# The tiles of the normed activations' high and low parts start 32 bytes further on

## The chip, the cores and the metric

The kernel runs on one core of a Trainium2 chip. The metric is the device time of one execution in microseconds; the times given are medians over runs. The core has a matrix engine (TensorE, in the profile PE for its matmuls and PEld for its weight loads), VectorE (DVE), ScalarE (ACT), GpSimd (POOL), and SyncE (SP), which issues most of the DMA transfers. All of them work on one on-chip memory of 128 partitions; a tile takes the same range of bytes in every partition.

## What is computed

The reference is one step of a trunk of two layers over 128 context tokens and 512 latent tokens of 1024 channels. The part that takes most of the time is the channel mixer at the end of each layer, which reads a table `u` and a table `v` of 16384 experts each:

```
h = rmsnorm(x, g_ffn) * (1 + scale) + shift
q = (h @ w_q).reshape(tokens, 8, 2, 128)            # 8 heads, 2 halves
s = einsum('thpc,hpnc->thpn', q, sub_keys)          # scores against 128 keys per half
sv, si = top_k(s, 16)
...                                                 # the best 16 pairs of keys: eidx, gates
act = gelu(einsum('thkd,td->thk', u[eidx], h))
x = x + gate * einsum('thk,thkd->td', gates * act, v[eidx])
```

Ahead of it layer 0 has an attention and a recurrence, fed by one projection of the normed activations, and layer 1 has a pooling mixer.

## The kernel before

Tokens lie along the free dimension: `xT` holds the 1024 channels as 8 blocks of 128 partitions, each with 640 tokens (128 context, 512 latent).

**Products in three parts.** Every large product is made with float32r operands split into a rounded high part and the low rest, as high x high, high x low and low x high (`PAIRS`, L367). The normed activations stand in two tiles, `hh` (high) and `hl` (low), 8 blocks of 640 tokens each; L496 to L500 write them. The weights are split as they come: `w_load` (L284) fetches 512 KB into `wr`, `w_hi` (L293) lets ACT write the high part `wh`, `w_lo` (L311) lets DVE or POOL write the rest `wl`. `mm3` (L369) goes through the 8 blocks of channels k, and for each k through the three pairs; the stationary operand is 128 columns of a weight tile, the moving operand a stretch of `hh` or `hl`.

**Where matmuls read `hh` and `hl`.**

- Projections in layer 0, output projection, pooling mixer, and the 16 query chunks of each channel mixer (L379, L528, L1397): moving operands of 320 tokens, two halves per weight column.
- The "U stage" of each channel mixer (L1546 to L1598): all 512 latent tokens are multiplied with all 16384 rows of `u`, 128 rows in each of 128 turns. A turn is 24 matmuls with 512 moving columns from `hh` and `hl`, summed in one bank (L1550). In half of the turns 16 pairs of small f16 matmuls (`pgm`, L1424, L1425) follow, which build the gate matrix out of one-hot rows that DVE and ACT make beside.
- The attention's value product (L893): here 128 columns of `hh` or `hl` are the stationary operand and 512 columns of a weight tile the moving one.

The "V stage" (L1617 to L1641) multiplies the gated activations, split into `wgh` and `wgl`, with `v`: 128 turns of 24 matmuls of 512 columns over 8 banks; its last turn (L1647 to L1650) goes bank by bank with the three pairs one after the other. It reads the gate matrix back into `gt_` in even groups of 8 turns and into the memory of `hl` in odd ones (L1510 to L1518), since the activations are no longer needed then.

**What sets the order.** In the U and V stages the loop itself is the order; each engine goes through its queue. In the other stages a planner (`Plan`) lists operations with estimated costs and writes them out in an order it searches for with a fixed seed; it knows nothing of addresses.

**Where the tiles lie.** Pool `pc` places its tiles in the order in which they are named, each padded to a multiple of 32 bytes. In the program of the kernel before, the starts are (bytes within a partition):

| tile | start | over a multiple of 64 | over a multiple of 512 |
|---|---|---|---|
| `hh`, `hl` | 51264, 71744 | 0 | 64 |
| `s8` (8 columns for the recurrence) | 92224 | 0 | 64 |
| `wr` (3), from pool `pw` | 92256, 96352, 100448 | 32 | 96 |
| `wh` (2), `wl` (2) | 104544, 108640; 112736, 116832 | 32 | 96 |
| `wh3`, `wl3` (third pair in the U and V stages) | 126560, 130656 | 32 | 96 |
| `gt_`, layers 0 and 1 | 192096, 181856 | 32 | 96 |
| `wgh`, layer 0 (2) | 212576, 214624 | 32 | 96 |
| `wgl`, layer 0 (2) | 216672, 218720 | 32 | 96 |

The `wgh` and `wgl` of layer 1 also stand 32 over a multiple of 64 and 96 over one of 512. Block k of `hh` starts 2560 k bytes on, its latent tokens 512 bytes later, its second half of 320 tokens 1280 bytes later, and the columns of a weight tile in steps of 512 bytes: all of these are multiples of 64, so that the third column of the table holds for every operand of these matmuls.

Of the kernel before, what the change touches and what calls it, by code (L numbers as in the profile page):

```python
# [11 lines left out]
F32 = mybir.dt.float32  # L12
# [144 lines left out]
def tile_trunk(ctx: ExitStack, tc: tile.TileContext, a, o):  # L157
# [5 lines left out]
    pc = ctx.enter_context(tc.tile_pool(name="pc", bufs=1))  # L163
# [12 lines left out]
    def col(name, j=None):  # L176
        s, w = COLS[name]
        return cols[:, s:s + w] if j is None else cols[:, s + j:s + j + 1]
# [57 lines left out]
    def norm_cols(l, part):  # L236
# [8 lines left out]
    perm = pc.tile([128, 128], F32, name="perm")  # L245
    eps = pc.tile([128, 1], F32, name="eps")
    warm = pc.tile([128, 1], F32, name="warm")
    G.iota(iota16, pattern=[[1, 128]], base=0, channel_multiplier=0,
           allow_small_or_imprecise_dtypes=True)
    G.memset(ones, 1.0)  # L250
# [293 lines left out]
    def lru_columns(pl):  # L544
        n = 8
        lam = col("lam")
        z = pl.tile([128, n], F32, name="lz")
        s = pl.tile([128, n], F32, name="ls")
        s2 = pl.tile([128, n], F32, name="ls2")
        q = pl.tile([128, n], F32, name="lq")  # L550
        S.activation(z, lam, AF.Abs)
        S.activation(z, z, AF.Exp, scale=-1.0)
        V.tensor_scalar(s, z, 2.0, None, op0=OP.add)
        V.reciprocal(s, s)
        V.tensor_tensor(s, s, z, op=OP.mult)
        V.tensor_tensor(s2, s, s, op=OP.mult)
        V.memset(q, 1.0 / 19)
        for k in range(8, -1, -1):
            V.tensor_tensor(q, q, s2, op=OP.mult)
            V.tensor_scalar(q, q, 1.0 / (2 * k + 1), None, op0=OP.add)  # L560
        V.tensor_tensor(q, q, s, op=OP.mult)
        V.tensor_scalar(s, lam, -1.0, 0.0, op0=OP.mult, op1=OP.max)
        s8 = pc.tile([128, n], F32, name="s8")
        V.scalar_tensor_tensor(s8, q, 2.0, s, op0=OP.mult, op1=OP.add)
        V.tensor_scalar(s8, s8, -8.0, None, op0=OP.mult)
        return s8

    def mixer0(p_mm, tmp, gt, firsts):
        NK = TP + 128 + TS
# [1104 lines left out]
    with tc.tile_pool(name="tmp", bufs=1) as tmp, tc.tile_pool(name="pmm", bufs=1, space=PSUM) as p_mm:  # L1674
        with tc.tile_pool(name="pm0", bufs=1) as pm0:
# [152 lines left out]
            for c in range(2):  # L1828
                wts.next()
            plan.run(S=1.5)  # L1830
            s8 = lru_columns(pm0)
        mixer0(p_mm, tmp, gt, firsts)
    A, B, gt = norm_cols(0, 1)
    peer(0, A, B, gt)
# [134 lines left out]
```

## Time and profile before

| | |
|---|---|
| median of 3 runs | 3773.19 us (3772.8 to 3774.68) |
| the profiled execution | 3772.78 us, of which its span is 3771.0 us |
| PE busy | 3622.1 us, 96% of the span |
| DVE busy | 2997.7 us, 79% |
| ACT, POOL busy | 1640.7 us, 828.3 us |
| granted clock of TensorE, mean | 0.98 |
| moved by DMA | 894.58 MB, mean 237 GB/s |

The profile is of one execution. Busy time is a union of spans; a matmul's span is longer than the distance to the next one, since they are pipelined, so what a stream of matmuls costs is read from the distance between starts. `idle before` is the time an engine stood still ahead of an instruction, with what ended it.

### The profile page before, as it was taken

How to read it: one execution, taken by the hardware profiler on the slowest of the kernel's cores; microseconds unless marked ns; L12 is line 12 of the kernel's file. 1: busy time of each engine (PE TensorE's matmuls, PEld its weight loads, DVE VectorE, ACT ScalarE, POOL GpSimd, SP SyncE). 2: the span in 40 equal slices, each digit the busy share in tenths (PEclk: the TensorE clock that was granted, in tenths of full speed). 3: DMA queues.
4: the chain of work that ended last, by engine and by line, in shares of the span. 5: the costliest groups of instructions: out<-in, count | busy, mean ns of one | idle time of the engine just before them, and what ended most of it. 6: DMA issues, size and time to landing. Idle time of an engine off the chain costs nothing. (4 is left out here: it accounts for less than half of the span.)

```text
span 3771.0 us, 52891 instructions
## 1 busy us (share of the span) xinstructions
PE 3622.1 (96%) x18190; PEld 2986.1 (79%) x18190; DVE 2997.7 (79%) x6901; ACT 1640.7 (44%) x2900; POOL 828.3 (22%) x673
## 2 busy tenths in 40 slices
PE   7989889999999999999996799999999999999997
PEld 5957888888888888888885797888888888888886
DVE  7876888888988778888887798988888656666665
ACT  3743323756657333333333323657566433333333
POOL 3122311111111412222213321111111322222221
PEclk9999899999999999999998899999999999999999
DMA  5233126878778999999991215878788978888883
GB/s 200 74 118 130 53 66 202 276 256 280 255 261 277 361 309 324 330 331 323 324 318 47 69 57 176 265 258 279 257 269 269 339 250 298 294 295 297 299 296 107
DMA packets 400162, 894.58 MB, mean 237 GB/s; under 512 B 33746, under 2 KB 170386, under 8 KB 399252
## 3 DMA queue, kind: packets, MB, share of 16 engines
q1 hardware_dynamic: 272884, 490.07, 40.5%
q0 software_dynamic: 74016, 271.09, 21.1%
q10 hardware_dynamic: 52992, 130.05, 8.8%
q8 instruction: 142, 2.33, 0.3%
q14 instruction: 128, 1.05, 0.1%
HBM read 758.26 MB, written 132.81 MB: 236 GB/s over the span
## 5 line engine op out<-in xcount | busy, mean ns | idle before, releaser
L315 DVE TENSOR_TENSOR wl<-wr,wh 128x1024 fp32r<-128x1024 f32 x544 | 660.4, 1215 | 546.7 <-ACT wh L306 470.5
L306 ACT ACTIVATE wh<-wr 128x1024 fp32r<-128x1024 f32 (+1 forms) x578 | 601.0, 1041 | 900.1 <-PE po L1632 735.8
L1288 POOL DMA_INDIRECT gat<-in_u_dram,idx x256 | 283.5, 1107 | 1285.4 <-DVE oh L1478 655.1
L1288 POOL DMA_INDIRECT gat<-in_v_dram,idx x256 | 303.6, 1186 | 1022.6 <-DVE accP L1610 957.4
L1632 PE MATMUL po<-wgh,wh 128*128 128x512 f32 x2032 | 501.9, 389 | 0.0
L1632 PE MATMUL po<-wgh,wl 128*128 128x512 f32 x2032 | 501.8, 389 | 0.0
L1632 PE MATMUL po<-wgl,wh 128*128 128x512 f32 x2032 | 501.8, 389 | 0.0
L1632 PEld LDWEIGHTS po<-wgh,wh 128*128 128x128 f32 x2032 | 381.4, 188 | 79.3
L1632 PEld LDWEIGHTS po<-wgl,wh 128*128 128x128 f32 x2032 | 381.4, 188 | 79.2
L1632 PEld LDWEIGHTS po<-wgh,wl 128*128 128x128 f32 x2032 | 381.4, 188 | 79.2
L1610 DVE SCALAR_TENSOR_TENSOR accP<-gat,aP,accP 128x1024 f32<-128x1024 f32 x254 | 324.8, 1279 | 0.5
L1480 DVE TENSOR_SCALAR oh<-iota,ij,gs 128x128 f16<-128x128 f16 x1024 | 321.9, 314 | 0.0
L1411 DVE SCALAR_TENSOR_TENSOR gat<-gat,hP 128x1024 f32<-128x1024 f32 x256 | 310.7, 1219 | 12.2 <-DMA gat<-in_u_dram,idx 12.2
L1419 ACT ACTIVATE oh<-oh,gs 128x128 f16<-128x128 f16 x1024 | 313.4, 387 | 0.0
L1478 DVE TENSOR_SCALAR oh<-iota,ij 128x128 f16<-128x128 f16 x1024 | 253.2, 247 | 0.0
L1542 ACT ACTIVATE wgh<-w 128x512 fp32r<-128x512 f32 x256 | 161.8, 632 | 206.6 <-PE po L1632 205.2
L1544 DVE TENSOR_TENSOR wgl<-w,wgh 128x512 fp32r<-128x512 f32 x256 | 174.9, 683 | 9.4 <-ACT wgh L1542 9.4
L1431 ACT ACTIVATE stag<-pgm 128x512 f32<-128x512 f32 x256 | 135.4, 578 | 0.0
L315 POOL TENSOR_TENSOR wl<-wr,wh 128x1024 fp32r<-128x1024 f32 (+2 forms) x34 | 72.6, 2136 | 276.3 <-ACT wh L306 276.3
L1424 PE MATMUL pgm<-oh 128*128 128x128 f16 x1024 | 129.5, 220 | 0.0
L1425 PE MATMUL pgm<-oh 128*128 128x128 f16 x1024 | 128.1, 219 | 0.0
L189 DVE SCALAR_TENSOR_TENSOR mjunk<-wm,silu 128x1024 f16<-128x1024 f32 x96 | 117.0, 1219 | 11.5 <-DMA gt__12588<-g_d 9.8
(2282 smaller groups left out, 7257.9 us busy)
## 6 DMA issues: line engine op xcount, KB each, us to landing
wr<-in_uT_dram SPq DMA_DIRECT2D x256, 512.0 KB, 4.4
wr<-in_v_dram SPq DMA_DIRECT2D x256, 512.0 KB, 4.5
g_d<-stag ACTq DMA_DIRECT2D x128, 512.0 KB, 6.3
act_d<-at ACTq DMA_DIRECT2D x240, 256.0 KB, 4.8
at<-act_d SPq DMA_DIRECT2D x240, 256.0 KB, 4.9
wm<-in_w_mod_dram SPq DMA_DIRECT2D x88, 512.0 KB, 7.3
hl<-g_d SPq DMA_DIRECT2D x128, 256.0 KB, 5.8
wr<-in_w_q_dram SPq DMA_DIRECT2D x32, 512.0 KB, 3.6
```

The costliest lines, as they stand in the source:

```text
L306: S.activation(hi[:, :n], RAW[i][:, :n], AF.Copy)
L315: (eng or (V if e == "v" else G)).tensor_tensor(lo[:, :n], RAW.pop(i)[:, :n], hi[:, :n], op=OP.subtract)
L1288: G.indirect_dma_start(out=r, out_offset=None, in_=a[f"u{l}" if s < 128 else f"v{l}"], in_offset=bass.IndirectOffsetOnAxis(ap=idx[:, s % 1 ...
L1411: V.scalar_tensor_tensor(ug, ug, 1.0, hP, op0=OP.mult, op1=OP.mult, accum_out=aP[:, s:s + 1])
L1419: S.activation(oh[:, 2], oh[:, 1], AF.Copy, scale=gr[:, tl:tl + 1])
L1431: S.activation(sg[:, :, t4:t4 + 4], pgm.rearrange("p q i -> p i q"), AF.Copy, scale=1.0 / GSCALE)
L1478: V.tensor_scalar(oh[:, 0], iota16, ij[:, 1, tl:tl + 1], None, op0=OP.is_equal)
L1480: V.tensor_scalar(oh[:, 1], iota16, ij[:, 0, tl:tl + 1], gs[:, 0, tl:tl + 1], op0=OP.is_equal, op1=OP.mult)
L1542: S.activation(wh, w32, AF.Copy)
L1544: return lambda: V.tensor_tensor(wl, w32, wh, op=OP.subtract)
L1610: V.scalar_tensor_tensor(accP, vg, aP[:, s:s + 1], accP, op0=OP.mult, op1=OP.add)
L1632: PE.matmul(po[d], (hi, lo)[x][:, d * 128:(d + 1) * 128], (wh, wl)[y], start=(n == 0 and p == 0), stop=False)
```

## The change

The tile `s8` is made together with the small constants, ahead of `hh` and `hl`, instead of inside `lru_columns`, which no longer returns it. `s8` has 128 x 8 float32, 32 bytes in a partition. So `hh` starts at 51296, `hl` at 71776 and `s8` at 51264; `wr` and all that follows start where they did. No instruction is added, removed or moved; those that name `hh`, `hl` or `s8` hold other addresses.

```
     warm = pc.tile([128, 1], F32, name="warm")
+    s8 = pc.tile([128, 8], F32, name="s8")
     G.iota(iota16, pattern=[[1, 128]], base=0, channel_multiplier=0,
...
         V.tensor_scalar(s, lam, -1.0, 0.0, op0=OP.mult, op1=OP.max)
-        s8 = pc.tile([128, n], F32, name="s8")
         V.scalar_tensor_tensor(s8, q, 2.0, s, op0=OP.mult, op1=OP.add)
         V.tensor_scalar(s8, s8, -8.0, None, op0=OP.mult)
-        return s8
...
-            s8 = lru_columns(pm0)
+            lru_columns(pm0)
```

## Rows read from the trace of the kernel before

**Rows 1.** The page, busy time of each engine: us, share, instructions.
```profile
PE 3622.1 (96%) x18190; PEld 2986.1 (79%) x18190; DVE 2997.7 (79%) x6901; ACT 1640.7 (44%) x2900; POOL 828.3 (22%) x673
```
**Rows 2.** Stretches: bounds, length, busy us (instructions) per engine, clock, DMA share, GB/s.
```profile
core 0: us, PE busy (x) PEld busy (x) DVE busy (x) ACT busy (x) POOL busy (x), PEclk, DMA share, GB/s
...
80.00:200.00 120.00, 117.34 (x712) 108.08 (x712) 105.41 (x136) 89.81 (x128) 19.21 (x17) 1.00 0.28 90
...
440.00:525.00 85.00, 85.00 (x608) 85.00 (x607) 78.15 (x399) 26.57 (x44) 24.02 (x10) 1.00 0.21 63
525.00:1340.00 815.00, 801.17 (x4201) 646.05 (x4200) 692.72 (x2063) 445.79 (x924) 153.79 (x134) 0.99 0.78 261
...
2330.00:3180.00 850.00, 849.95 (x4429) 687.94 (x4428) 686.79 (x1864) 459.48 (x939) 168.98 (x154) 1.00 0.82 275
```
**Rows 3.** Timeline, PE, two whole U turns: start us, length, engine, line, operands.
```profile
596.11 0.40 PE L373 MATMUL pu__4928<-hh,wh 128*128 128x512 f32 x1
596.34 0.40 PE L373 MATMUL pu__4928<-hl,wh 128*128 128x512 f32 x1
596.58 0.40 PE L373 MATMUL pu__4928<-hh,wl 128*128 128x512 f32 x1
...
607.31 0.40 PE L373 MATMUL pu__5029<-hh,wh 128*128 128x512 f32 x1
```
**Rows 4.** Timeline, PE, V stage, runs of 8 matmuls.
```profile
1501.17 1.98 PE L1632 MATMUL po<-wgl,wh 128*128 128x512 f32 x8
...
1521.12 1.98 PE L1632 MATMUL po<-wgh,wh 128*128 128x512 f32 x8
```
**Rows 5.** Timeline, PE, last V turn, bank by bank.
```profile
2021.60 0.39 PE L1649 MATMUL po<-wgh,wh 128*128 128x512 f32 x1
2021.83 0.39 PE L1649 MATMUL po<-wgl,wh 128*128 128x512 f32 x1
...
2023.41 0.39 PE L1649 MATMUL po<-wgh,wl 128*128 128x512 f32 x1
...
2025.45 0.39 PE L1649 MATMUL po<-wgl,wh 128*128 128x512 f32 x1
...
2026.84 0.39 PE L1649 MATMUL po<-wgl,wh 128*128 128x512 f32 x1
...
2027.75 0.39 PE L1649 MATMUL po<-wgh,wl 128*128 128x512 f32 x1
```
**Rows 6.** Timeline, PE, value product of the attention.
```profile
256.45 0.39 PE L373 MATMUL pv__2069<-wh,hh 128*128 128x512 f32 x1
...
260.42 0.39 PE L373 MATMUL pv__2091<-wh,hl 128*128 128x512 f32 x1
```
**Rows 7.** Stretches of the two U stages, matmuls of L373 alone.
```profile
560.00:1330.50 770.50, 723.95 (x3036) 1.00 0.81 270
2276.00:3047.00 771.00, 724.45 (x3036) 1.00 0.79 264
```
**Rows 8.** Groups by line: small matmuls of the gate matrix: count, busy us, mean ns.
```profile
L1424 PE MATMUL pgm<-oh 128*128 128x128 f16 x1024 | 129.5, 220 | 0.0
```
**Rows 9.** Timeline, PE, from the small matmuls into a U turn.
```profile
709.68 0.22 PE L1425 MATMUL pgm<-oh 128*128 128x128 f16 x1
709.71 0.47 PE L373 MATMUL pu__6163<-hh,wh 128*128 128x512 f32 x1
710.02 0.39 PE L373 MATMUL pu__6163<-hl,wh 128*128 128x512 f32 x1
```
**Rows 10.** Stretches of the first U stage, columns as in Rows 2.
```profile
640.00:696.00 56.00, 55.95 (x293) 44.75 (x292) 53.90 (x149) 32.96 (x75) 12.56 (x11) 1.00 0.81 253
696.00:768.00 72.00, 72.00 (x443) 58.08 (x440) 60.54 (x215) 52.12 (x124) 9.90 (x11) 1.00 0.83 283
1246.00:1330.00 84.00, 84.00 (x362) 67.63 (x361) 67.66 (x100) 24.50 (x31) 36.71 (x24) 1.00 0.99 372
```
**Rows 11.** Timeline, PE, query chunk with 320 columns, runs of 2.
```profile
477.90 0.46 PE L373 MATMUL pp<-hh,wh 128*128 128x320 f32 x2
...
480.25 0.46 PE L373 MATMUL pp<-hh,wl 128*128 128x320 f32 x2
```
**Rows 12.** Groups by line and shape: ACT writes to weight and activation tiles.
```profile
L306 ACT ACTIVATE wh<-wr 128x1024 fp32r<-128x1024 f32 x560 | 593.1, 1060 | 894.9 <-PE po L1632 732.8 <-ACT at L1556 77.5 <-DMA wr<-in_uT_dram 35.3
...
L497 ACT ACTIVATE hh<-xn 128x640 fp32r<-128x640 f32 x20 | 14.7, 737 | 33.6 <-DVE xn L493 33.4
```
**Rows 13.** DMA issues: operands, KB each, median us to landing.
```profile
hl<-g_d SPq DMA_DIRECT2D x128, 256.0 KB, 5.8
...
gt__13596<-g_d SPq DMA_DIRECT2D x8, 256.0 KB, 6.2
```

More of the change, by code (lines that the diff above doesn't have):

```diff
@@ L247, in tile_trunk @@
     warm = pc.tile([128, 1], F32, name="warm")
+    s8 = pc.tile([128, 8], F32, name="s8")
     G.iota(iota16, pattern=[[1, 128]], base=0, channel_multiplier=0,
@@ L562, in lru_columns @@
         V.tensor_scalar(s, lam, -1.0, 0.0, op0=OP.mult, op1=OP.max)
-        s8 = pc.tile([128, n], F32, name="s8")
         V.scalar_tensor_tensor(s8, q, 2.0, s, op0=OP.mult, op1=OP.add)
         V.tensor_scalar(s8, s8, -8.0, None, op0=OP.mult)
-        return s8
     def mixer0(p_mm, tmp, gt, firsts):
@@ L1830, in tile_trunk @@
             plan.run(S=1.5)
-            s8 = lru_columns(pm0)
+            lru_columns(pm0)
         mixer0(p_mm, tmp, gt, firsts)
```

## The prediction

> **What bounds the kernel now.** First read the busy times of the page: PE 96%, with its weight loads beside it, DVE 79%, ACT 44% [rows 1]. Then the table of stretches: from 2330 to 3180 us, in layer 1's U stage and the start of its V stage, PE is busy 849.95 of 850 us at full granted clock, in layer 0's U stage 801 of 815, in its query chunks 85 of 85 [rows 2]. There the time is the number of matmuls times the distance between their starts. So the third view is the timeline of PE, read for distances.
>
> Two streams of the same form (128 x 128 stationary, 512 moving columns, float32r) run at two distances. In the U stage two turns, 48 matmuls, take 607.31 - 596.11 = 11.20 us, 0.2333 us each [rows 3]. In the V stage 88 matmuls take 1521.12 - 1501.17 = 19.95 us, 0.2267 us each [rows 4]. Both run without a gap at clock 1.00, and the weights lie in the same tiles. The difference is 6.6 ns, 2.8%.
>
> What differs between the streams? Not the order of the pairs and not the bank: the last V turn goes pair by pair within one bank as the U stage does, and its 8 distances from 2021.60 to 2023.41 give 0.2263 us [rows 5]. What is left is where the operands lie. In V the moving operand and the weights both start 32 bytes over a multiple of 64; in U the moving operand starts on a multiple of 64 and the weights 32 over. The value product swaps the roles, `hh` and `hl` being stationary: the same mismatch, and 17 distances take 260.42 - 256.45 = 3.97 us, 0.2335 us [rows 6]. So in this trace mismatch goes with 0.2333 us and match with 0.2267 us, whichever operand is which. After the change `hh` and `hl` stand 32 over a multiple of 64 (96 over one of 512), as all weights and V's operands do.
>
> **The change part by part.** No instruction, DMA or wait is added or removed and nothing changes its place in a queue. What can change is the length of those that read or write `hh`, `hl` or `s8`.
>
> *U matmuls.* The two windows hold 3036 matmuls each [rows 7], 6072 or 253 turns (the first turn of each stage falls partly or wholly outside). The small matmuls come 8 per turn on each of L1424 and L1425, x1024 in all [rows 8]: 128 turns have them, 125 have not. A turn without them should gain 24 x 6.6 = 0.159 us: 125 x 0.159 = 19.9 us. After small matmuls the stream has to settle: the first distance is 710.02 - 709.71 = 0.31 us anyway [rows 9], and in the last V turn, whose operands match, the 6 distances after an interruption (2025.45 to 2026.84) are still 1.39 / 6 = 0.232 us before the next 4 drop to 0.91 / 4 = 0.2275 us [rows 5]. So I give such a turn 24 - 7 = 17 matmuls: 128 x 17 x 6.6 ns = 14.4 us. Together 34.3 us; the ends are nothing, and 24 per turn, 253 x 0.159 = 40.2 us.
>
> *What is late next.* DVE makes the low weights and the one-hot rows. In turns with small matmuls it is busy 60.54 of 72 us [rows 10], 16% of air, so the gain passes. While it picks the 16 best of the next group of tokens it is busy 53.90 of 56 us [rows 10]: 4% of air for a gain of 2.8%, with its work in lumps. There are four groups per layer; at some 6 turns each that is 48 turns at 0.14 us; I take half as lost, 3.4 us (ends 0 and 6.7). In the last 84 us of the first U stage the DMA share is already 0.99 at 372 GB/s [rows 10]; transfers can't go faster, so I count its 15 turns as no gain: 15 x 0.159 = 2.4 us (ends 0 and 2.4). PE is then held by weights in the place of its own pace. 34.3 - 3.4 - 2.4 = 28.5 us.
>
> *Value product.* 36 matmuls x 6.6 ns = 0.2 us.
>
> *Products with 320 columns.* 2796 of them read `hh` or `hl` (1020 on L379, 432 on L528, 1344 on L373, counted from the loops). They run at (480.25 - 477.90) / 16 = 0.1469 us, mismatched [rows 11]; no row shows them matched. The slope from there to V's 512 columns is (0.2267 - 0.1469) / 192 = 0.416 ns per column, which is one column per cycle at the 2.4 GHz level of the clock; over that, V stands 13.4 ns, the narrow products 13.6 and U 20.0. The narrow ones are thus at V's overhead already, and I take no change. Ends: one step of 6.6 ns less (0.1403) or more (0.1535), 2796 x 6.6 ns = 18.5 us, of which some 60%, 11 us, stands where PE has hardly a gap (L379 and the query chunks, [rows 2]).
>
> *Writes and other reads.* `hh` is written by ACT at 737 ns for 640 columns, 1.15 ns per column; `wh`, already 32 over a multiple of 64, at 1060 ns for 1024, 1.04 ns [rows 12]. A start at 32 shows no price. I take zero for these 28 writes and the 28 of the low parts; the difference of the two rates, 0.11 ns x 640 = 71 ns, bounds it to 56 x 71 ns = 4 us either way. The gate matrix comes into `hl` in 5.8 us, into `gt_` (already 32 over) in 6.2 us [rows 13]. If `hl` took the 0.4 us more, it would fall on the last of 8 pieces alone, 16 groups x 0.4 = 6.4 us were nothing in front; but the product made from it goes to PE only a turn (24 x 0.2267 = 5.4 us) later, and that hides it: zero. `s8` is read 16 times as a column: nothing.
>
> Sum: 28.5 + 0.2 = 28.7 us off the profiled 3772.78 us, 3744.1; the median of the runs lies 0.4 us above the profiled execution, so 3744.5 us.
>
> **The rivals.**
>
> *Narrow ones gain too.* If mismatch costs every float32r stream a step, the 320-column products fall to 0.1403 us: another 11 us, 3733 us. For it: in the U stage and in the value product mismatch had its price every time. Against: their overhead is V's already [rows 4, 11].
>
> *Nothing happens.* The two paces could come from something else that sets `hh` apart: its place low in memory, a tile that is walked in 8 blocks. The value product, which reads the same tiles, fits that as well [rows 6]. Against it: every block k and both tiles give the same distance, though they lie far apart. Then 3773 us. The Trainium skill speaks for this rival: "SBUF — State Buffer", section "Who interferes with whom", gives the matmul's moving operand and the weight load read ports of their own and says that PE never waits on anyone. By that rule no address can matter and the time stays 3773 us; but by it U and V should also run at one pace, and the rows show two.
>
> *It gets slower.* A moving operand that starts on a multiple of 64 may be the cheap case in itself, and the U stage slow for another reason. Then 32 bytes on costs one more step: U at 0.2400 us, 6072 x 6.6 ns = 40 us, and 11 us of narrow products: 3824 us. It decides from the point where U's distance rises by 7.5 us / 6072 = 1.2 ns. For it: `hh` and `hl` are the only matmul operands of the three-part products on a multiple of 64. Against it: the fastest wide stream of the kernel, V's, starts 32 over [rows 4].
>
> **How the numbers follow.** Forecast 0.61; narrow ones too 0.14; nothing 0.17; slower 0.08. A measurement of this kernel tells 0.2% (7.5 us) from no change. Forecast and narrow gain lie below that line, so faster is 0.75, same 0.17, slower 0.08. The forecast's own range is 3730 (full gain in all turns, little lost) to 3760 (half of it); it joins the second case below, to 3722, and "nothing" above, to 3775. What is left out is the slower case and the far ends.
>
> **What would show it.** In the trace after: 48 U matmuls of turns without small ones take 10.88 us, not 11.20; after small ones 5 to 7 distances near 0.232 us, then 0.2267; the value product at 0.2267; the V stage as before at 0.2267; the narrow products at 0.147 (forecast) or 0.140 us (first rival). PE gaps should appear in the last turns of the first U stage and where DVE picks the best 16. It is wrong if U stays at 0.2333 us, if gaps eat more than a fifth of the gain, or if any of V's or DVE's lengths move.

## The result, and the profile after

The changed kernel takes 3744.23 us (median of 4 runs, 3741.04 to 3745.06), the kernel before 3772.99 us beside it (4 runs, 3772.27 to 3774.68): ratio 0.9922, interval 0.9904 to 0.9939. The forecast was 3744.5. The profiled execution took 3744.72 us (its span is 3743.0), 28.06 us less than the profiled one of before.

The page of the changed kernel, busy time of each engine (compare [rows 1]):

```profile
PE 3589.5 (96%) x18190; PEld 2984.0 (80%) x18190; DVE 2996.6 (80%) x6901; ACT 1645.0 (44%) x2900; POOL 836.7 (22%) x673
```

PE is 32.6 us less busy with the same 18190 matmuls; DVE, ACT and the weight loads are about as busy as they were. It is the matmuls that changed. The timeline of PE, two whole U turns of the changed kernel (start, length, engine, line, operands; compare [rows 3]):

```profile
595.12 0.39 PE L374 MATMUL pu__4928<-hh,wh 128*128 128x512 f32 x1
...
606.00 0.39 PE L374 MATMUL pu__5029<-hh,wh 128*128 128x512 f32 x1
```

48 distances take 10.88 us, 0.2267 us each; before they took 11.20. The V stage of the changed kernel, 88 matmuls apart (compare [rows 4]):

```profile
1487.20 1.98 PE L1631 MATMUL po<-wgl,wh 128*128 128x512 f32 x8
...
1507.15 1.98 PE L1631 MATMUL po<-wgh,wh 128*128 128x512 f32 x8
```

Again 19.95 us, 0.2267 us: V kept its pace and U came down to it. The value product and a query chunk of the changed kernel (compare [rows 6, 11]):

```profile
256.99 0.39 PE L374 MATMUL pv__2069<-wl,hh 128*128 128x512 f32 x1
...
260.62 0.39 PE L374 MATMUL pv__2091<-wh,hl 128*128 128x512 f32 x1
```

```profile
477.98 0.46 PE L374 MATMUL pp<-hh,wh 128*128 128x320 f32 x2
...
480.32 0.46 PE L374 MATMUL pp<-hh,wl 128*128 128x320 f32 x2
```

16 distances of the value product take 3.63 us, 0.2269 each. The query chunk's 16 take 2.34 us, 0.1463 where there were 0.1469, a difference of 0.01 us over the 16: the products of 320 columns don't gain. And a turn that follows small matmuls (compare [rows 9]):

```profile
707.80 0.22 PE L1424 MATMUL pgm<-oh 128*128 128x128 f16 x1
707.83 0.48 PE L374 MATMUL pu__6163<-hh,wh 128*128 128x512 f32 x1
708.14 0.40 PE L374 MATMUL pu__6163<-hl,wh 128*128 128x512 f32 x1
...
710.23 0.39 PE L374 MATMUL pu__6163<-hl,wh 128*128 128x512 f32 x1
...
713.18 0.39 PE L374 MATMUL pu__6163<-hh,wl 128*128 128x512 f32 x1
713.41 0.23 PE L1423 MATMUL pgm<-oh 128*128 128x128 f16 x1
...
714.28 0.48 PE L374 MATMUL pu__6252<-hh,wh 128*128 128x512 f32 x1
```

The first distance is 0.31 us, the next 9 take 710.23 - 708.14 = 2.09 us (0.2322 each), and only the last 13 run at (713.18 - 710.23) / 13 = 0.2269. The turn lasts 714.28 - 707.83 = 6.45 us. Before, it began at 709.71 [rows 9] and the next one here, so it lasted 6.55:

```profile
716.26 0.47 PE L373 MATMUL pu__6252<-hh,wh 128*128 128x512 f32 x1
```

One thing is new. The waits of PE in the first U stage of the changed kernel (who waited <- for whom: us in total, times, longest):

```profile
PE pu__4613 L374 <- DVE wl L316: 9.8, 1, 9.8
PE pu__4579 L374 <- DVE wl L316: 3.1, 1, 3.1
PE pt__5336 L1458 <- DVE fj L1268: 1.8, 1, 1.8
```

From the timelines of PE and DVE, the first transpose of that group and DVE's last step for `fj`, before and then changed:

```profile
652.11 0.27 PE L1459 MATMUL pt__5336<-identf,fi 128*128 128x128 f32 x1
650.09 2.28 DVE L1269 TENSOR_REDUCE fj<-eq 128x128 f32<-128x2048 f16 x1
```

```profile
649.52 0.27 PE L1458 MATMUL pt__5336<-identf,fi 128*128 128x128 f32 x1
649.26 2.28 DVE L1268 TENSOR_REDUCE fj<-eq 128x128 f32<-128x2048 f16 x1
```

The first two waits stand at the start of the stage and were there before (9.7 and 2.9 us). The third is new: the transposes of the first group's indices come due 2.6 us earlier, DVE has `fj` only 0.8 us earlier, and PE stands 1.8 us. The turn ahead of them lasts 7.72 us in the place of 6.11; in the second U stage it is 7.70.

### The profile page after: what moved, and what is told of

It is laid out like the page before. It is cut to its first block, busy times and chain, and to the rows that moved or that the text cites. A ratio compares the mean times of both kernels' runs of the same rounds, so it can differ in the third digit from the quotient of the medians.

```text
span 3743.0 us, 52891 instructions
## 1 busy us (share of the span) xinstructions
PE 3589.5 (96%) x18190; PEld 2984.0 (80%) x18190; DVE 2996.6 (80%) x6901; ACT 1645.0 (44%) x2900; POOL 836.7 (22%) x673
## 5 line engine op out<-in xcount | busy, mean ns | idle before, releaser
L1287 POOL DMA_INDIRECT gat<-in_u_dram,idx x256 | 292.5, 1143 | 1252.8 <-DVE oh L1477 643.3
```

Source lines behind the costliest of these rows:

```text
L1287: G.indirect_dma_start(out=r, out_offset=None, in_=a[f"u{l}" if s < 128 else f"v{l}"], in_offset=bass.IndirectOffsetOnAxis(ap=idx[:, s % 1 ...
```

## The experiments

Theory before the runs: a wide float32r matmul (512 columns) loses one step of 6.6 ns where its moving operand and its weights start at unequal remainders modulo 64. Rivals: the place of the moving operand alone decides; the place of `hh` and `hl` alone decides; the grid is coarser. Each edit is made to the changed kernel and only puts unused bytes between tiles, unless it is said otherwise. "Apart" is the start of the weights less that of `hh`, modulo 512, read from the program. Distances are of turns without small matmuls; medians stand beside 3772.3 to 3773.0 for the kernel before in the same series.

| kernel | `hh` / weights, over a multiple of 512 | apart | U, us | V, us | median, us |
|---|---|---|---|---|---|
| before | 64 / 96 | 32 | 0.2333 | 0.2267 | 3772.99 |
| changed | 96 / 96 | 0 | 0.2267 | 0.2267 | 3744.23 |
| both_0 | 128 / 128 | 0 | 0.2267 | 0.2267 | 3745.38 |
| w_0 | 96 / 128 | 32 | 0.2333 | 0.2267 | 3772.89 |
| w_64_on | 96 / 160 | 64 | 0.2333 | 0.2267 | 3773.90 |
| w_128_on | 96 / 224 | 128 | 0.2333 or 0.2324 | 0.2267 | 3770.58 |
| w_256_on | 96 / 352 | 256 | 0.2267 | 0.2267 | 3744.67 |
| v_apart | 96 / 96, `wgh` 128 | 0, in V 32 | 0.2267 | 0.2334 | 3785.63 |

**both_0.** Everything moves on by 32 bytes together.

```
     s8 = pc.tile([128, 8], F32, name="s8")
+    pc.tile([128, 8], F32, name="pad0")
```

> From the changed kernel, 32 more bytes of nothing ahead of hh: hh, hl, all weights and V's operands now start on a multiple of 64. Theory (a wide float32r matmul loses one step of 6.6 ns when its moving operand and its weights start at unequal remainders modulo 64): U and V both at 0.2267 us, 3744 us. Rival (a moving operand 32 over a multiple of 64 is fast in itself): U and V both 0.2333 us, 2 x 6144 matmuls, 3773 + 41 = 3814 us. Second rival (each start off a multiple of 64 costs something of its own): U and V below 0.2267, at 0.2200 us by one step, about 3664 us.

3745.38 us, ratio to before 0.9929 (0.9913 to 0.9946). PE, both_0, two U turns:

```profile
597.90 0.39 PE L375 MATMUL pu__4966<-hh,wh 128*128 128x512 f32 x1
...
608.78 0.39 PE L375 MATMUL pu__5077<-hh,wh 128*128 128x512 f32 x1
```

10.88 us for 48. U and V are both on multiples of 64 and both at 0.2267 us: it is not 32 over that is fast, and being on the multiple is not faster either. Both rivals fall.

**w_0.** The weights move, `hh` and `hl` stay where the change put them.

```
     hl = pc.tile([128, KD, T], F32R, name="hl")
+    pc.tile([128, 8], F32, name="pad1")
```

> From the changed kernel, 32 bytes of nothing behind hl: hh and hl stay 32 over a multiple of 64, all weights and V's moving operands start on one. Theory (unequal remainders modulo 64): U 0.2333, value product 0.2333, V 0.2267 us, 3773 us. Rival (place of the moving operand alone, fast at 32 over): U 0.2267, V 0.2333 us, 3744 + 41 = 3785 us. Second rival (place of hh and hl in memory, whatever the weights): U 0.2267, V 0.2267, 3744 us.

3772.89 us, ratio 1.0001 (0.9991 to 1.001). PE, w_0, two U turns:

```profile
596.94 0.40 PE L375 MATMUL pu__4929<-hh,wh 128*128 128x512 f32 x1
...
608.14 0.40 PE L375 MATMUL pu__5030<-hh,wh 128*128 128x512 f32 x1
```

11.20 us: with `hh` and `hl` at the addresses of the changed kernel the whole gain is gone. The price belongs to the pair of operands and to no tile. Whether a matmul's own weights count or those that are loaded during it, no run tells, since all weight tiles have one remainder.

**w_64_on.** 64 bytes behind `hl` (`[128, 16]` in the pad above).

> From the changed kernel, 64 bytes of nothing behind hl: hh and hl start 96 over a multiple of 128, the weights 32 over one; the remainders modulo 64 are equal. Theory (equal modulo 64 is enough): U 0.2267 us, 3744 us. Rival (the grid is 128 bytes or coarser; in the changed kernel all starts are equal modulo 512): U 0.2333 us, 3773 us.

3773.90 us, ratio 1.0003 (0.9993 to 1.0013). PE, w_64_on, two U turns:

```profile
594.90 0.39 PE L375 MATMUL pu__4929<-hh,wh 128*128 128x512 f32 x1
...
606.10 0.39 PE L375 MATMUL pu__5030<-hh,wh 128*128 128x512 f32 x1
```

11.20 us, though the remainders modulo 64 are equal. My theory falls in this form: 64 is not the grid. The value product of the same run, where the weights move and `hh` and `hl` are stationary, shows something else:

```profile
255.42 0.39 PE L375 MATMUL pv__2070<-wh,hh 128*128 128x512 f32 x1
...
259.31 0.40 PE L375 MATMUL pv__2092<-wh,hl 128*128 128x512 f32 x1
```

17 distances take 3.89 us, 0.2288 each: with the roles swapped, 64 bytes apart cost a third of the step.

**w_128_on, w_256_on.** 128 and 256 bytes behind `hl` (`[128, 32]`, `[128, 64]`).

> From the changed kernel, 128 bytes of nothing behind hl: the starts of hh and hl and those of the weights now differ by 128 modulo 512. A difference of 64 was slow (3774 us), so the remainder modulo 64 is not what counts; the theory is equal remainders on a coarser grid. Grid of 128 bytes: U 0.2267 us, 3744 us. Grid of 256 or 512 bytes: U 0.2333 us, 3773 us.

> From the changed kernel, 256 bytes of nothing behind hl: starts differ by 256 modulo 512. Grid of 128 or 256 bytes: U 0.2267 us, 3744 us. Grid of 512 bytes: U 0.2333 us, 3773 us. A coarser one is excluded by V, where the weights of the 8 banks lie 512 bytes apart and all run at 0.2267 us.

128 apart: 3770.58 us, ratio 0.9997 (0.9987 to 1.0006). 256 apart: 3744.67 us, ratio 0.9925 (0.9909 to 0.9942). PE, two U turns, w_128_on and then w_256_on:

```profile
595.81 0.39 PE L375 MATMUL pu__4929<-hh,wh 128*128 128x512 f32 x1
...
607.01 0.39 PE L375 MATMUL pu__5030<-hh,wh 128*128 128x512 f32 x1
```

```profile
597.99 0.39 PE L375 MATMUL pu__4966<-hh,wh 128*128 128x512 f32 x1
...
608.87 0.39 PE L375 MATMUL pu__5077<-hh,wh 128*128 128x512 f32 x1
```

11.20 and 10.88 us. But w_128_on doesn't keep this pace everywhere. 15 turns without small matmuls in its second U stage:

```profile
2278.00 0.39 PE L375 MATMUL pu__20876<-hh,wh 128*128 128x512 f32 x1
...
2361.66 0.40 PE L375 MATMUL pu__21572<-hh,wh 128*128 128x512 f32 x1
```

360 distances take 83.66 us, 0.2324 each, five sixths of the step. Of the distances tried, 0 and 256 are free, and 32, 64 and 128 cost something; the weights of V's 8 banks, 512 bytes from one to the next, all run at 0.2267 us as well. So wherever the starts agree modulo 256 the stream is fast, and wherever they didn't it was slower, but not always by a whole step. Other distances were not tried.

**v_apart.** The same fault, put into the stage that had none: V's moving operands move on by 32 bytes.

```
+                if n == 0:
+                    pv.tile([128, 8], F32, name="padv")
                 wh = pv.tile([128, TS], F32R, name="wgh", tag="wgh", bufs=2)
```

> From the changed kernel, 32 bytes of nothing ahead of wgh, so that V's moving operands (wgh, wgl) start 128 over a multiple of 512 and the weights stay 96 over; the U stage is left as it is. Theory (unequal starts of moving operand and weights cost a wide float32r matmul one step): V goes from 0.2267 to 0.2333 us, 6144 x 6.6 ns = 41 us, 3785 us. Rival (the price belongs to hh and hl, their place or the walk over 8 blocks): V stays at 0.2267 us, 3744 us.

3785.63 us, ratio 1.0032 (1.0022 to 1.0043), 41.4 us more than the changed kernel. PE, v_apart, V stage, 88 matmuls apart:

```profile
1486.91 2.03 PE L1633 MATMUL po<-wgl,wh 128*128 128x512 f32 x8
...
1507.45 2.03 PE L1633 MATMUL po<-wgh,wh 128*128 128x512 f32 x8
```

20.54 us, 0.2334 each, and U stays at 0.2267 us. The step can be put into either stage at will, and V pays it in full: 6144 x 6.6 ns = 41 us.

**hl_only, hl_alone.** One of three matmuls apart. In hl_only `hl` has 32 bytes ahead and 32 behind; only after w_64_on was it plain that this leaves `hh` apart too (96 against 160, and `hl` 128), so it says nothing of one odd matmul among equal ones. hl_alone mends that with 480 bytes behind:

```
+    pc.tile([128, 8], F32, name="pad0")
     hl = pc.tile([128, KD, T], F32R, name="hl")
+    pc.tile([128, 120], F32, name="pad1")
```

> From the changed kernel, 32 bytes ahead of hl and 32 behind it: hh and the weights 32 over a multiple of 64, hl on one, so that one of three U matmuls (weights high, activations low) has unequal remainders. Theory, priced per matmul: the distance that belongs to the hl matmul is 6.6 ns longer, mean 0.2289 us, a third of the 28.8 us comes back, 3754 us. Rival (the step is paid wherever two neighbouring matmuls' moving operands differ too): two of three, mean 0.2311, 3763 us. Rival (only hh counts): 3744 us.

> From the changed kernel, 32 bytes of nothing ahead of hl and 480 behind it: hh and the weights 96 over a multiple of 512 as in the changed kernel, hl alone 128 over. One of three U matmuls has unequal starts. Priced per matmul: 0.2267, 0.2267 and 0.2333 us, mean 0.2289, 3754 us. Rival (one odd matmul sets the pace of its neighbours too): 0.2311 to 0.2333 us, 3763 to 3773 us.

hl_only 3762.38 us (ratio 0.9971, 0.9962 to 0.9981), hl_alone 3766.16 us (0.9982, 0.9972 to 0.9991). PE, hl_only, five turns without small matmuls, and then hl_alone, two turns that follow small matmuls, the same 15 distances in each:

```profile
773.37 0.39 PE L376 MATMUL pu__7000<-hh,wh 128*128 128x512 f32 x1
...
801.11 0.39 PE L376 MATMUL pu__7220<-hh,wh 128*128 128x512 f32 x1
```

```profile
724.78 0.40 PE L376 MATMUL pu__6346<-hl,wh 128*128 128x512 f32 x1
...
728.25 0.40 PE L376 MATMUL pu__6346<-hl,wh 128*128 128x512 f32 x1
...
731.30 0.40 PE L376 MATMUL pu__6435<-hl,wh 128*128 128x512 f32 x1
...
734.80 0.40 PE L376 MATMUL pu__6435<-hl,wh 128*128 128x512 f32 x1
```

In hl_alone the 15 distances take 3.47 and 3.50 us: 0.231 and 0.233 us per matmul, turn by turn, from one and the same mixture. The price per matmul (0.2289) does not hold: one odd matmul in three takes some two thirds of the step or the whole of it, and which of the two seems to be settled where the stream begins anew, for a turn keeps its pace to its end. The mixture is not the cause of the lower pace, though. In hl_only all three pairs are apart (64, 32 and 64 bytes), so that by the rule so far U should stand at 0.2333 and the kernel near 3773 us; yet its 120 distances take 27.74 us, 0.231 each, and the kernel takes 3762.38 (the first rival's 3763, but that one had `hh` equal to the weights). Together with w_128_on and the value product of w_64_on this leaves the size of the price open: apart is slower, by a third of the step to the whole of it, and by what rule, no run here shows.

**split_small.** The 16 small matmuls of a turn, 8 in the middle and 8 at the end.

```
+                    if k == 3 and m:
+                        mm_group(m[0])
...
-                m = drain(1, mm_group)
+                for q in m[1:]:
+                    mm_group(q)
```

> From the changed kernel, the two groups of 8 small matmuls of a turn stand in two places (behind block k = 3 and behind the last) in the place of one. Theory (each interruption of the wide stream has a price of its own: a first distance of 0.314 us where 0.227 would do, then 9 distances of 0.2322 us, in all 0.087 + 9 x 0.0055 = 0.137 us): 128 more interruptions, 17.5 us, 3762 us. Rival (the price goes by the number of small matmuls, which stays): 3744 us.

3763.80 us, ratio 0.9977 (0.9966 to 0.9988). PE, split_small, the middle of a turn:

```profile
711.14 0.39 PE L380 MATMUL pu__6163<-hh,wl 128*128 128x512 f32 x1
711.37 0.23 PE L1423 MATMUL pgm<-oh 128*128 128x128 f16 x1
...
711.80 0.48 PE L380 MATMUL pu__6163<-hh,wh 128*128 128x512 f32 x1
712.11 0.40 PE L380 MATMUL pu__6163<-hl,wh 128*128 128x512 f32 x1
```

The first distance and the slow ones come back after every interruption. A section of 18 turns, 16 of them with small matmuls, lasts 116.04 us against 114.12 in the changed kernel: 1.92 / 16 = 0.12 us for each, where 0.137 was expected. Over 128 that is 15.4 us, and the profiled execution (3760.67 us) is 15.95 us longer than the changed kernel's; the medians differ by 19.6 us, more than these interruptions explain.

**pair_small, block_1, pair_block.** Two ways to more, from what the runs so far had shown, and both together.

```
-                m = drain(1, mm_group)
+                m = drain(1, mm_group) if len(stages[1]) > 2 or not g else []
```

```
+                    if tt == 1:
+                        yield "block"
                     pp = bank("pt_")
```

> From the changed kernel, the small matmuls of two turns are held back and issued together behind every second turn (32 at once): 64 interruptions fewer. Theory (0.137 us for each): 8.8 us less, 3735 us. Rival (24 one-hot buffers are 6 groups; DVE must now wait for PE to release them, falls behind with the weights' low parts, and PE waits for those): no gain or slower than 3744 us, with PE gaps in the turns that follow.

> From the changed kernel, the three transposes of the first group of tokens are queued on PE one turn later. In the changed kernel PE waits 1.8 us there for DVE's fj, once per layer. Theory (this wait is what the faster U stream lost at DVE, and it has a turn of air): the wait goes and nothing takes its place, 2 x 1.8 = 3.6 us less, 3740.6 us. Rival (DVE's backlog only shifts, PE waits for the weights' low parts or at the next groups instead): 3744 us.

> The edits of pair_small and block_1 together. Theory (the interruptions of the wide stream at 0.12 us each and the wait of 1.8 us per layer for fj are separate terms): pair_small's 3738.5 us less 2 x 1.8 us, at most less some 1 us given back at the end of the first U stage as in block_1: 3735 to 3736.5 us. Rival (both draw on the same air of DVE, so that the second adds nothing): 3738.5 us.

pair_small: 3738.54 us (3736.91 to 3741.39), ratio 0.9908 (0.9893 to 0.9923), 5.7 us under the changed kernel where 8.8 were expected. A section of 18 turns lasts 113.16 us, 0.96 less for 8 interruptions fewer, again 0.12 each; over 64 that is 7.7 us. In its trace 3.6 of them are given back: 1.95 in the last 16 turns of the first U stage, 1.6 in the turn behind the first transposes of the second. block_1: 3742.30 us (3740.91 to 3744.53), ratio 0.9919 (0.9906 to 0.9933); the runs alone don't set it apart from the changed kernel. In its trace the transposes come a turn later and PE no longer waits:

```profile
657.48 0.27 PE L1460 MATMUL pt__5373<-identf,fi 128*128 128x128 f32 x1
657.59 0.27 PE L1460 MATMUL pt__5373<-identf,fj 128*128 128x128 f32 x1
657.70 0.27 PE L1460 MATMUL pt__5373<-identf,fg 128*128 128x128 f32 x1
657.73 0.48 PE L374 MATMUL pu__5420<-hh,wh 128*128 128x512 f32 x1
```

From the turn in which PE waited to the end of the stage, the second U stage is 2.0 us shorter than in the changed kernel, the first 1.1 (it gives 0.9 back in its last turns, as pair_small does). pair_block: 3733.46 us (3731.65 to 3735.17), ratio 0.9899 (0.9882 to 0.9915), the best version here, 10.8 us under the changed kernel. Its U stages are 5.1 and 6.3 us shorter than those of the changed kernel, 11.4 together; the two terms make 7.7 + 3.6 = 11.3. That is more than I gave it: of the 3.6 us that pair_small lost, 0.8 are left, at the end of the first U stage. The waits of PE in the first U stage of pair_block:

```profile
PE pu__4613 L374 <- DVE wl L316: 9.6, 1, 9.6
PE pu__4579 L374 <- DVE wl L316: 3.0, 1, 3.0
PE pu__12849 L374 <- DVE wl L316: 0.4, 1, 0.4
```

## Why the prediction was right, point by point

The time came out within 0.3 us, closer than the runs of one kernel lie together (4 us) and closer than the terms were right; that much of it is luck. The two U stages, from their first to their last wide matmul, give 13.96 us (797.18 to 783.22) and 14.00 us (797.55 to 783.55) of the 28.06.

- **What separates the two paces.** Right that it is where moving operand and weights start with respect to each other, and that at 32 bytes apart it doesn't matter which is which (value product, w_0, v_apart). Wrong in the grid: "a multiple of 64" was the coarsest that I looked at, and w_64_on disproves it. The forecast held because the change makes the starts agree modulo 512, and so modulo 256; the prediction states this in passing but doesn't rest on it, so that here too it had luck. By its own rule the layout of w_64_on would have done as well, and that one gains nothing.
- **Plain turns**, 0.159 us each. 15 of them in a row went from 84.00 to 81.60 us: 0.160.
- **Turns after small matmuls**, 0.112 us each. It was 0.10 (6.55 to 6.45): the stream settles after 10 distances, not 7. A section of 18 turns gained 1.95 us, not 2.11; over 8 sections, 1.3 us less than counted.
- **DVE**, 3.4 us off. 3.2 us came off, but in another way than I had it: not half of the gain wherever the 16 best are picked (the turns between the groups gained 0.98 us in 7), but one wait of PE per layer, at the first group.
- **DMA at the end of the first U stage**, 2.4 us off. This term was mis-sized. The last 16 turns went from 89.67 to 87.43 us, 2.24 gained, where those of the second stage gained 2.49: a loss of 0.25 us, in two turns of 5.56 and 5.58 us. A DMA share of 0.99 [rows 10] was no wall: PE drew ahead by 2.2 us and mostly found its weights there, while the transfers over the same turns rose from 371 to 376 GB/s. (The 16 turns counted are those ahead of the stage's last one.) In block_1 and pair_small, where PE is further ahead there, some 0.9 and 1.95 us are lost. The waits that the profile names there are for DVE's low weights (0.8 us at most, in pair_small); that the transfers are behind them is not shown.
- **Not counted**: the first two turns of each stage, where PE waits for the low weights, lost 0.15 us in all, where the forecast had counted one of the four as a gain (0.3 us); the turn that now waits for `fj` lost its own gain as well, once per layer (0.3 us); turns that begin behind the last small matmuls of a group or run into the next transposes gained 0.1 and not 0.16 us (0.9 us). Together: 28.7 - 1.3 + 0.2 + 2.15 - 1.5 = 28.25 us, against 28.06 in the trace. Losses put too high (2.35 us) and gains put too high (2.8 us) nearly cancel.
- **Narrow products, writes, `hl` as gate matrix**: zero, as forecast. Outside the two U stages the whole kernel gained 0.10 us, and the value product is part of that.
- **The rivals.** "Nothing happens" drew on the Trainium skill, "SBUF — State Buffer", section "Who interferes with whom", by which PE's two reads are independent and PE waits for no one. That no address can matter is what I made of it; the page does not say so. The measurement decides against that reading for this form: w_0 and v_apart change nothing but addresses, and the pace of the wide stream changes by 2.9%. "It gets slower" is excluded by the result itself, and both_0 adds that a start on a multiple of 64 is not the cheap case. "Narrow ones gain too" is excluded by their 0.1463 us.

## What to carry to other kernels

Where one stream of matmuls runs slower than another of the same form and neither has gaps, compare the starts of moving operand and weights modulo 256 bytes before anything else: 32 unused bytes in the right place were worth 28 us, and in the wrong place cost 41. A tile of odd size that is named in a new place shifts all that follow, so the starts should be looked at after every such edit. And each interruption of the wide stream by small matmuls cost some 0.12 us here: they are better issued together, though pair_small gave 3.6 of its 7.7 us back elsewhere in the stage.

## What had not been expected of the hardware

Starts that agree modulo 256 bytes gave 0.2267 us in every run. Starts that don't gave no single pace: 0.2333 us at 32 bytes apart wherever it was looked at, 0.2333 at 64 in U but 0.2288 in the value product of the same run, 0.2333 and 0.2324 at 128, and about 0.231 or 0.233 with mixtures, which change from turn to turn in hl_alone. The price falls on 512 columns and not on 320: those take 0.145 to 0.147 us on average at any distance tried. What in the chip makes 256 bytes the grid, what sets the size of the price, and why narrow streams don't feel it, stays open.
